# Differential attention of a hybrid block: scores of two heads in one burst, small tiles turned by DMA, and another order of the second half's projections

## The chip, the cores and the metric

The kernel runs on one core of a Trainium2 chip. Its metric is the device time of one execution in microseconds (us). The profile is one execution taken by the hardware profiler. Its engines are called PE (TensorE, matmuls), PEld (TensorE's weight loads), DVE (VectorE), ACT (ScalarE), POOL (GpSimd) and SP (SyncE, which here only issues DMAs).

## The reference

Two layers work on 272 tokens (16 learned "meta" tokens and 256 of the input) with 1024 features. Each layer has a mixer with three branches, retention (4 heads), HGRN2 (8 heads) and differential attention (8 heads), and a feed-forward part with a short convolution. All projections come from one matrix. The part that matters here, cut:

```python
q = rope(q.reshape(b, l, 2 * DA_HEADS, DA_DH), pos).reshape(b, l, DA_HEADS, 2, DA_DH) * DA_DH ** -0.5
k = rope(k.reshape(b, l, 2 * DA_HEADS, DA_DH), pos).reshape(b, l, DA_HEADS, 2, DA_DH)
...
    s = jnp.einsum('bqhmd,bkhmd->bhmqk', qb, k)
    p = jax.nn.softmax(jnp.where(allowed, s, MASK_VALUE), axis=-1)
    w = p[:, :, 0] - lam * p[:, :, 1]
    return jnp.einsum('bhqk,bkhe->bqhe', w, v)
...
o = _rms(o) * subln_g.astype(F32) * (1.0 - lambda_init)
...
y_b = jnp.einsum('blnc,ncd->blnd', branches, w_branch.astype(F32))
y = jnp.sum(gates * y_b, axis=2)
```

So each of eight heads has two score maps (m = 0, 1) with 64 features each. Their softmaxes are subtracted with a factor, and the difference weighs 128 values per head.

## The kernel before, in words

**Main stream.** Activations lie with features on the partitions and the 272 tokens along the columns (258 in most of layer 1, whose first 14 tokens are needed only as keys). Every projection is a stream of 128x128 weight tiles. `products` (L926) takes a pair of output tiles (16 weight tiles) at a time. Each weight tile is cut by `_Weights.next` (L652) into a high part `whi` (cast by ACT) and a rest `wlo` (subtraction on DVE), and costs three matmuls (L953 to L955): high by high, low by high, high by low. Weights come in chunks of eight tiles over SP's queue into three `wraw` buffers; `whi` and `wlo` have four buffers each.

**Order of the main stream.** `ORDER` (L65) lists the pairs of every layer by name: hq, hf, hi, hg for HGRN2, rq, rk, rv, rg for retention, dq, dk, dv for attention, m0 to m2 for the branch gates, b0 to b2 for the branch products, wo, fi, fo. Marks stand between them: "+daa" and "+dab" are the places where the work of attention's first and second half (four heads each) joins, "!da" is the place by which it is meant to be done, "*b0" to "*b2" split a branch's output into high and low parts (tiles b0hi, b0lo and so on). Before the change the second half's part reads dq, dq, b0, b0, dk, dk, dv, dv, "+dab".

**Side work.** All else is added to a planner (`_Plan`, L356) as operations with an engine, an estimated cost and a key (the wanted place, in units of main stream time). `behind` (L1476) gathers the operations of one job, `in_turn` makes buffers of a tag be taken in the job's order, and `settle` (L1491) spreads the keys of the jobs from their joining to the mark. `behind(..., 2, 8)` lets a job begin after the operation eight from the end of the job three places before it in the chain. `order` (L456) then runs a greedy simulation, one queue for each engine, and fixes the order of instructions. A main matmul is never moved before another; side matmuls go between them. An operation starts at most 12 units before its key.

**Buffers.** The main products use two PSUM tiles ("main"). Side matmuls use two banks of tag "bank" and two of tag "acc". Tags of small buffers: "two_a", "two_b" (score maps, 2 each), "wts" (2), "vsrc" (4, shared by the 16-bit planes "apart" and "turned" and by the values before they are turned), "dm" (2).

**Attention.** `da_first` (L1362) computes the first 16 rows of all four heads at once: scores "ds" from a block-diagonal q, softmax, both maps combined into `w`, and a matmul "wt" with a constant that turns and sums the maps into `dw`. `da_head` (L1392) does one head: it takes a "wts" buffer a1 and copies its part of `dw` there, computes the scores of 256 rows into two "bank" tiles (four matmuls over 64 rows each, two of 272 and two of 144 columns, L1405 to L1411), adds the mask and takes the maximum on DVE, exponentials on ACT, combines the maps on DVE, turns the 32-bit result by two DMA transposes (ACT copies the 16-bit halves apart, SP issues the two transposes, ACT copies them back to a1), and multiplies by the values ("do"). The last 16 columns of the two row blocks are gathered in `dt`. `da_tail` (L1458) turns `dt` by a TensorE transpose ("wt"), and multiplies by the tail values `dvs`. Then b2hi and b2lo are made of the output `da`.

**Tails of the values.** `tail_tokens` (L1020) turns the last 16 tokens of rv, hi and dv by a TensorE transpose into a bank ("vm"), and ACT copies them to "vs". It is called five times in a layer (rv once, hi twice, dv twice).

Of the kernel before, what the change touches and what calls it, by code (L numbers as in the profile page):

```python
# [15 lines left out]
U16 = mybir.dt.uint16  # L16
# [5 lines left out]
P = 128  # L22
# [36 lines left out]
def _pairs(name, lo, hi):  # L59
# [16 lines left out]
    + _pairs("dq", 2, 4) + _pairs("b0", 0, 2) + _pairs("dk", 2, 4) + _pairs("dv", 2, 4)  # L76
    + [("+dab", 0)]
# [617 lines left out]
def _trace(ctx, tc, plan, a, depth, probe):  # L695
# [323 lines left out]

    def tail_tokens(tails):  # L1020

        pm = bank("vm")
        pe.transpose(pm[:, :P], tails, ident)
        vs = temp(P, "vs", 4)
        act.activation(vs, pm[:, :P], AF.Copy)
        return vs
# [40 lines left out]
    for li in range(depth):  # L1067
# [294 lines left out]
        def da_first(b):  # L1362
# [11 lines left out]
            pool.memset(w, 0.0)  # L1374
            s = bank("ds")
# [10 lines left out]
            wt = bank("wt")  # L1386
            pe.matmul(wt[:, : 4 * META], w, const[:, C_SUM:C_MAP], start=True, stop=True)
            st[f"dw{b}"] = temp(4 * META, "am", 3)
            act.activation(st[f"dw{b}"], wt[:, : 4 * META], AF.Copy)
            st[f"dt{b}"], st[f"do{b}"] = (temp(P, n, 1).rearrange("p (g h t) -> p g h t", g=2, h=4) for n in ("dt", "dot"))  # L1390

        def da_head(b, hd):  # L1392
            q, k, vt, out = st[f"dq{b}"], st[f"dk{b}"], st[f"dvt{b}"], st[f"da{b}"]
            scale = DA_DH ** -0.5

            a1 = temp(T + P + TAIL, "wts")
            act.activation(a1[:, :META], st[f"dw{b}"][:, hd * META : (hd + 1) * META], AF.Copy)
            tiles = ((META + P, T, 0), (META, META + P, T))
            sb = [temp(2 * T, tag) for tag in ("two_a", "two_b")]
            ss = [bank("ds") for _ in range(2)]  # L1400
            red = temp(12, "dm")
            nm, sm, cf = (red[:, 4 * i : 4 * i + 4].rearrange("p (t m) -> p t m", m=2) for i in range(3))


            def scores():  # L1405
                for q0, nk, at in tiles:
                    for m in range(2):
                        half = slice(64 * m, 64 * m + 64)
                        nc.tensor.matmul(ss[m][:, at : at + nk], q[half, hd, q0 : q0 + P], k[half, hd, :nk], start=True, stop=True)  # L1409

            plan.add("pe", scores, 0.95, [x[:, : T + P + META] for x in ss], [q[:, hd, :], k[:, hd, :]])  # L1411
            plan.hold(*sb, a1)
            for i, (q0, nk, at) in enumerate(tiles):
                mask = const[:, C_MASK + T - nk : C_MASK + T]
                for m in range(2):
# [175 lines left out]
        for name, j in ORDER:  # L1591
# [8 lines left out]
            elif name in ("+daa", "+dab"):  # L1600
# [3 lines left out]
                for hd in range(4):  # L1604
                    behind(lambda: da_head(b, hd), "da", 2, 8)
# [174 lines left out]
```

## Time and profile before

| | before |
|---|---|
| median of 3 runs (lowest to highest) | 1275.9 us (1275.59 to 1276.77) |
| the profiled execution | 1275.23 us |
| its span, first to last instruction | 1273.4 us |
| mean granted TensorE clock | 0.999 |
| ACT, whi: cast of a chunk of 1024 columns | 1056 ns, 399 of them |
| DVE, wlo: rest of a chunk | 1239 ns, 399 of them |
| DMA transposes issued by SP | 86 |
| weight loads issued by SP, 512 KB each | 402 |

In a row of groups stand the source line, engine and operation, then the tile written and the tiles read (buffer numbers left out), the shape, the count, busy time in us and mean ns of one, and the idle time of the engine just before them with what ended it. L633 is the line of the helper through which all side work is recorded, so side work is told apart by its tiles. In a row of a timeline stand start and duration in us. A matmul of 32-bit data over 128 rows appears as two records, a main matmul or a transpose as one. Ends of matmuls are modelled, starts are recorded. In a row of waits stand the total, the number and the longest.

### The profile page before, as it was taken

The numbers are of one execution on the slowest core, as the hardware profiler recorded it, in microseconds if no ns is written. First come the engines' busy times: TensorE is split into PE (matmuls) and PEld (weight loads), VectorE is DVE, ScalarE is ACT, GpSimd is POOL, SyncE is SP. The second block draws the span as 40 slices with busy tenths as digits, with TensorE's granted clock in tenths as the row PEclk, the third lists the DMA queues.
The fourth block names the chain that finished last, engine by engine and source line by source line (L and its number), as shares of the span: only waits on it lengthen the run. The fifth ranks groups of instructions, "written<-read, shape, count | busy, mean of one in ns | idle before, by whom it ended". The sixth has DMA issues, their size and how long they took to land.

```text
span 1273.4 us, 28668 instructions
## 1 busy us (share of the span) xinstructions
PE 1264.0 (99%) x11626; PEld 1242.9 (98%) x11626; DVE 964.7 (76%) x1669; ACT 886.0 (70%) x1638; POOL 113.3 (9%) x89
## 2 busy tenths in 40 slices
PE   9999999999999999999999999999999999999998
PEld 8999999999999999999999999999999999999986
DVE  6787587898776789786576875869987867898854
ACT  6766677758798576665456567877588975787643
POOL 2000031201111000000010000411011120000000
PEclk9999999999999999999999999999999999999999
DMA  8655547655746546556555545576557466476663
GB/s 269 197 167 158 160 149 227 165 169 147 213 132 208 182 150 199 178 170 190 176 182 182 167 144 187 149 217 186 166 147 227 146 209 196 150 224 204 208 197 108
DMA packets 103444, 229.29 MB, mean 180 GB/s; under 512 B 49552, under 2 KB 49680, under 8 KB 103312
## 3 DMA queue, kind: packets, MB, share of 16 engines
q1 hardware_dynamic: 103024, 226.94, 57.1%
q8 instruction: 91, 1.49, 0.5%
q10 hardware_dynamic: 288, 0.52, 0.1%
q14 instruction: 41, 0.34, 0.1%
HBM read 216.16 MB, written 1.05 MB: 171 GB/s over the span
## 4 chain that ended last, share of the span: by engine, by line
PE 98%; DVE 1%; ACT 0%; DMA 0%; issue 0%; SPq 0%; ACTq 0%
PE main L953 28%; PE main L954 28%; PE main L955 28%; PE fo L1566 2%; PE fo L1564 2%; PE fo L1565 2%; PE lev L1160 1%; PE fi L955 1%; PE fi L954 1%; PE fi L953 1%; PE ds L1409 1%; PE s L633 0%; DMA h<-in_h 0%; PE do L633 0%; PE ro L633 0%; PE px L633 0%
## 5 line engine op out<-in xcount | busy, mean ns | idle before, releaser
L953 PE MATMUL main<-xh,whi 128*128 128x272 f32 (+1 forms) x2240 | 644.1, 288 | 1.6 <-ACT whi L633 1.1
L633 DVE TENSOR_TENSOR wlo<-wraw,whi 128x1024 fp32r<-128x1024 f32 (+1 forms) x411 | 500.2, 1222 | 182.0 <-ACT whi L633 180.5
L955 PE MATMUL main<-xh,wlo 128*128 128x272 f32 (+1 forms) x2240 | 636.8, 284 | 0.4 <-DVE wlo L633 0.4
L954 PE MATMUL main<-xl,whi 128*128 128x272 f32 (+1 forms) x2240 | 636.5, 284 | 0.0
L633 ACT ACTIVATE whi<-wraw 128x1024 fp32r<-128x1024 f32 (+1 forms) x411 | 426.2, 1041 | 202.3 <-PE main L954 99.4
L953 PEld LDWEIGHTS main<-xh,whi 128*128 128x128 f32 x2240 | 421.8, 188 | 2.7 <-ACT whi L633 1.3
L955 PEld LDWEIGHTS main<-xh,wlo 128*128 128x128 f32 x2240 | 421.7, 188 | 1.1 <-DVE wlo L633 0.9
L954 PEld LDWEIGHTS main<-xl,whi 128*128 128x128 f32 x2240 | 421.8, 188 | 0.7 <-issue 0.6
L633 POOL PARTITION_ALL_REDUCE hr<-hsq x36 | 75.1, 2106 | 448.8 <-ACT hsq L633 329.1
L633 DVE SCALAR_TENSOR_TENSOR two_b<-main,small,two_b 128x256 f32<-128x256 f32 (+2 forms) x128 | 54.4, 484 | 27.4 <-ACT two_b L633 27.3
L633 ACT ACTIVATE two_b<-main,small 128x272 f32<-128x272 f32 (+1 forms) x64 | 33.1, 566 | 26.8 <-PE main L955 26.5
L953 PE MATMUL main<-ghi,whi 128*128 128x272 f32 x176 | 50.8, 289 | 0.0
L954 PE MATMUL main<-glo,whi 128*128 128x272 f32 x176 | 50.6, 287 | 0.0
L955 PE MATMUL main<-ghi,wlo 128*128 128x272 f32 x176 | 50.3, 286 | 0.0
L953 PE MATMUL main<-b0hi,whi 128*128 128x272 f32 (+1 forms) x128 | 37.4, 292 | 0.0
L953 PE MATMUL main<-b1hi,whi 128*128 128x272 f32 (+1 forms) x128 | 37.1, 290 | 0.0
L953 PE MATMUL main<-yhi,whi 128*128 128x272 f32 (+1 forms) x128 | 36.4, 284 | 0.0
L955 PE MATMUL main<-yhi,wlo 128*128 128x272 f32 (+1 forms) x128 | 36.3, 284 | 0.0
L954 PE MATMUL main<-b0lo,whi 128*128 128x272 f32 (+1 forms) x128 | 36.3, 284 | 0.0
L954 PE MATMUL main<-ylo,whi 128*128 128x272 f32 (+1 forms) x128 | 36.3, 284 | 0.0
L955 PE MATMUL main<-b1hi,wlo 128*128 128x272 f32 (+1 forms) x128 | 36.3, 284 | 0.0
L954 PE MATMUL main<-b1lo,whi 128*128 128x272 f32 (+1 forms) x128 | 36.3, 284 | 0.0
(275 smaller groups left out, 2144.3 us busy)
## 6 DMA issues: line engine op xcount, KB each, us to landing
wraw<-in_w SPq DMA_DIRECT2D x402, 512.0 KB, 3.8
turned<-apart SPq DMA_TRANSPOSE x86, 2.5
h<-in_h SPq DMA_DIRECT2D x4, 272.0 KB, 5.4
dec<-in_dec SPq DMA_DIRECT2D x2, 544.0 KB, 5.7
wraw<-in_w SPq DMA_DIRECT2D x4, 256.0 KB, 5.0
const<-in_const SPq DMA_DIRECT2D x1, 937.0 KB, 7.7
gain<-in_gl SPq DMA_DIRECT2D x1, 512.0 KB, 4.4
out<-y ACTq DMA_DIRECT2D x2, 256.0 KB, 2.6
```

The lines of the kernel that those rows point to most:

```text
L633: self.plan.add(self.name, lambda: f(*args, **kw), cost, outs, ins, kind)
L953: nc.tensor.matmul(o, wh, hi, start=first, stop=False)
L954: nc.tensor.matmul(o, wh, lo, start=False, stop=False)
L955: nc.tensor.matmul(o, wl, hi, start=False, stop=last)
L1160: nc.tensor.matmul(o, keys, x, start=True, stop=True)
L1409: nc.tensor.matmul(ss[m][:, at : at + nk], q[half, hd, q0 : q0 + P], k[half, hd, :nk], start=True, stop=True)
L1564: nc.tensor.matmul(o, gh, wh, start=first, stop=False)
L1565: nc.tensor.matmul(o, gl, wh, start=False, stop=False)
L1566: nc.tensor.matmul(o, gh, wl, start=False, stop=end)
```

## The change

- `flip` is new: it turns a 128x128 tile of 32-bit values with two ACT copies that take the 16-bit halves apart, two DMA transposes issued by SP, and two ACT copies back. It needs one "vsrc" buffer.
- `tail_tokens` uses it in place of the TensorE transpose and the copy from PSUM. `da_first` uses it in place of the matmul "wt", with a DVE addition of the two maps behind it. `da_tail` uses it in place of the TensorE transpose. That makes 18 flips: ten in `tail_tokens`, four in `da_first`, four in `da_tail`.
- `da_head` becomes `da_pair`: the scores of two heads are one operation of eight matmuls (planned at 1.75 in place of 0.95 for one head) into two "bank" and two "acc" tiles. The maxima of both heads follow, then `da_rest` for each head. The "wts" buffer a1 is taken in `da_rest`, after the maps are combined, and no longer before the scores.
- `ORDER`: the second half reads dv, dv, dq, dq, dk, dk, "+dab", b0, b0.

```diff
--- before.py
+++ after.py
@@ -73,8 +73,8 @@
     + _pairs("dq", 0, 2) + _pairs("dv", 0, 2)
     + _pairs("dk", 0, 2)
     + [("+daa", 0), ("*b0", 0), ("!ret", 0)]
-    + _pairs("dq", 2, 4) + _pairs("b0", 0, 2) + _pairs("dk", 2, 4) + _pairs("dv", 2, 4)
-    + [("+dab", 0)]
+    + _pairs("dv", 2, 4) + _pairs("dq", 2, 4) + _pairs("dk", 2, 4)
+    + [("+dab", 0)] + _pairs("b0", 0, 2)
     + _pairs("b0", 2, 4) + _pairs("m1", 0, 4)
     + [("*b1", 0)]
     + _pairs("b1", 0, 4)
@@ -1017,12 +1017,23 @@
             act.activation(halves(top[2][:, cols].unsqueeze(1), i), turned[:, i, 1:2, :], AF.Copy)
         split(top[0][:, cols], top[1][:, cols], whole)
 
+    def flip(out, x):
+
+        t = planes("turned", 2 * P)
+        apart, turned = (t[:, i].rearrange("p (i x) -> p i x", i=2) for i in range(2))
+        halves = lambda t, i: t.bitcast(U16).rearrange("p (x two) -> p x two", two=2)[:, :, i]
+        for i in range(2):
+            act.activation(apart[:, i], halves(x, i), AF.Copy)
+        for i in range(2):
+            sync.dma_start(turned[:, i].rearrange("p (b x) -> p b x", x=P), apart[:, i], transpose=True)
+        for i in range(2):
+            act.activation(halves(out, i), turned[:, i], AF.Copy)
+
     def tail_tokens(tails):
 
-        pm = bank("vm")
-        pe.transpose(pm[:, :P], tails, ident)
         vs = temp(P, "vs", 4)
-        act.activation(vs, pm[:, :P], AF.Copy)
+        plan.key += 1.0
+        flip(vs, tails)
         return vs
 
     def inverse(r, sq, n):
@@ -1372,6 +1383,7 @@
                 half = slice(64 * m, 64 * m + 64)
                 act.activation(qs.rearrange("p (h m q) -> p h m q", h=4, m=2)[half, :, m, :], q[half, :, :META], AF.Copy)
             pool.memset(w, 0.0)
+            turned = x[:, T : T + P]
             s = bank("ds")
             pe.matmul(s[:, : 4 * META].rearrange("p (h k) -> p h k", h=4), qs, k[:, :, :META], start=True, stop=True)
             dve.tensor_tensor_reduce(out=p, in0=s[:, : 4 * META], in1=const[:, C_FIRST:C_SUM], scale=1.0,
@@ -1383,40 +1395,48 @@
 
             dve.tensor_reduce(out=w[:, :META], in_=p.rearrange("p (h k) -> p k h", h=4), axis=mybir.AxisListType.X, op=ADD)
             ts(w[:, :META], w[:, :META], cf, None, MUL)
-            wt = bank("wt")
-            pe.matmul(wt[:, : 4 * META], w, const[:, C_SUM:C_MAP], start=True, stop=True)
+            flip(turned, w)
+            maps = turned.rearrange("p (h m q) -> p h m q", h=4, m=2)
             st[f"dw{b}"] = temp(4 * META, "am", 3)
-            act.activation(st[f"dw{b}"], wt[:, : 4 * META], AF.Copy)
+            tt(st[f"dw{b}"].rearrange("p (h q) -> p h q", h=4), maps[:, :, 0, :], maps[:, :, 1, :], ADD)
             st[f"dt{b}"], st[f"do{b}"] = (temp(P, n, 1).rearrange("p (g h t) -> p g h t", g=2, h=4) for n in ("dt", "dot"))
 
-        def da_head(b, hd):
-            q, k, vt, out = st[f"dq{b}"], st[f"dk{b}"], st[f"dvt{b}"], st[f"da{b}"]
+        def da_scores(b, heads):
+            q, k = st[f"dq{b}"], st[f"dk{b}"]
+            banks = [[bank("ds") for _ in range(2)], [acc_bank("ds") for _ in range(2)]]
+            sb = [[temp(2 * T, tag) for tag in ("two_a", "two_b")] for _ in heads]
+            tiles = ((META + P, T, 0), (META, META + P, T))
+
+            def scores():
+                for hd, ss in zip(heads, banks):
+                    for q0, nk, at in tiles:
+                        for m in range(2):
+                            half = slice(64 * m, 64 * m + 64)
+                            nc.tensor.matmul(ss[m][:, at : at + nk], q[half, hd, q0 : q0 + P], k[half, hd, :nk], start=True, stop=True)
+
+            plan.add("pe", scores, 1.75, [x[:, : T + P + META] for ss in banks for x in ss],
+                     [x[:, hd, :] for x in (q, k) for hd in heads])
+            plan.hold(*sum(sb, []))
+            return [(ss, p, temp(12, "dm")) for ss, p in zip(banks, sb)]
+
+        def da_pair(b, heads):
             scale = DA_DH ** -0.5
-
-            a1 = temp(T + P + TAIL, "wts")
-            act.activation(a1[:, :META], st[f"dw{b}"][:, hd * META : (hd + 1) * META], AF.Copy)
             tiles = ((META + P, T, 0), (META, META + P, T))
-            sb = [temp(2 * T, tag) for tag in ("two_a", "two_b")]
-            ss = [bank("ds") for _ in range(2)]
-            red = temp(12, "dm")
-            nm, sm, cf = (red[:, 4 * i : 4 * i + 4].rearrange("p (t m) -> p t m", m=2) for i in range(3))
-
-
-            def scores():
-                for q0, nk, at in tiles:
-                    for m in range(2):
-                        half = slice(64 * m, 64 * m + 64)
-                        nc.tensor.matmul(ss[m][:, at : at + nk], q[half, hd, q0 : q0 + P], k[half, hd, :nk], start=True, stop=True)
-
-            plan.add("pe", scores, 0.95, [x[:, : T + P + META] for x in ss], [q[:, hd, :], k[:, hd, :]])
-            plan.hold(*sb, a1)
-            for i, (q0, nk, at) in enumerate(tiles):
-                mask = const[:, C_MASK + T - nk : C_MASK + T]
-                for m in range(2):
-                    cols = slice(at, at + nk)
+            pairs = [(i, m, slice(at, at + nk)) for i, (_, nk, at) in enumerate(tiles) for m in range(2)]
+            lanes = da_scores(b, heads)
+            parts = [[red[:, 4 * i : 4 * i + 4].rearrange("p (t m) -> p t m", m=2) for i in range(3)] for _, _, red in lanes]
+            for (ss, sb, _), (nm, _, _) in zip(lanes, parts):
+                for i, m, cols in pairs:
+                    mask = const[:, C_MASK + T - (cols.stop - cols.start) : C_MASK + T]
                     dve.tensor_tensor_reduce(out=sb[m][:, cols], in0=ss[m][:, cols], in1=mask, scale=1.0,
                                              scalar=-3e38, op0=ADD, op1=ALU.max, accum_out=nm[:, i, m : m + 1])
-            ts(nm, nm, -scale, None, MUL)
+                ts(nm, nm, -scale, None, MUL)
+            for hd, (_, sb, _), (nm, sm, cf) in zip(heads, lanes, parts):
+                da_rest(b, hd, sb, nm, sm, cf, tiles)
+
+        def da_rest(b, hd, sb, nm, sm, cf, tiles):
+            vt, out = st[f"dvt{b}"], st[f"da{b}"]
+            scale = DA_DH ** -0.5
             for i, (q0, nk, at) in enumerate(tiles):
                 for m in range(2):
                     p = sb[m][:, at : at + nk]
@@ -1428,6 +1448,8 @@
                 ts(p1, p1, cf[:, i, 1:2], None, MUL)
                 stt(p0, p0, cf[:, i, 0:1], p1, MUL, ADD)
             w = sb[0]
+            a1 = temp(T + P + TAIL, "wts")
+            act.activation(a1[:, :META], st[f"dw{b}"][:, hd * META : (hd + 1) * META], AF.Copy)
             apart, turned = planes("apart", 3 * P), planes("turned", 3 * P)
             halves = lambda t, i: t.bitcast(U16).rearrange("p (x two) -> p x two", two=2)[:, :, i]
             for i in range(2):
@@ -1458,11 +1480,11 @@
         def da_tail(b):
 
             o, out = st[f"do{b}"].rearrange("p g h t -> p (g h t)"), st[f"da{b}"]
-            wt = bank("wt")
-            pe.transpose(wt[:, :P], st[f"dt{b}"].rearrange("p g h t -> p (g h t)"), ident)
+            turned = temp(P, "tails")
+            flip(turned, st[f"dt{b}"].rearrange("p g h t -> p (g h t)"))
             w = temp(P, "tw")
             blocks = lambda t: t.rearrange("p (h t) -> p h t", t=TAIL)
-            tt(blocks(w), pair(wt[:, P - TAIL : P], 8), blocks(const[:, C_OWN : C_OWN + P]), MUL)
+            tt(blocks(w), pair(turned[:, P - TAIL : P], 8), blocks(const[:, C_OWN : C_OWN + P]), MUL)
             x = acc_bank("do")[:, :P]
             pe.matmul(x, st[f"dvs{b}"], w, start=True, stop=True)
             tt(o, o, x, ADD)
@@ -1601,8 +1623,8 @@
                 b = "ab".index(name[3])
                 st[f"da{b}"] = slot4("da")
                 behind(lambda: da_first(b), "da", 2)
-                for hd in range(4):
-                    behind(lambda: da_head(b, hd), "da", 2, 8)
+                for g in range(2):
+                    behind(lambda: da_pair(b, (2 * g, 2 * g + 1)), "da", 2, 8)
                 behind(lambda: da_tail(b), "da", 2)
             elif name[0] == "!":
                 settle(name[1:])
```

## The prediction

> **What bounds the kernel now.** I read first the page's busy shares and the chain that ended last, then the costliest groups with the idle time before them, then the timeline of TensorE around single interruptions of its main stream.
>
> ```profile
> span 1273.4 us, 28668 instructions
> ...
> PE 1264.0 (99%) x11626; PEld 1242.9 (98%) x11626; DVE 964.7 (76%) x1669; ACT 886.0 (70%) x1638; POOL 113.3 (9%) x89
> ...
> PE 98%; DVE 1%; ACT 0%; DMA 0%; issue 0%; SPq 0%; ACTq 0%
> ...
> L953 PE MATMUL main<-xh,whi 128*128 128x272 f32 (+1 forms) x2240 | 644.1, 288 | 1.6 <-ACT whi L633 1.1
> ...
> L955 PE MATMUL main<-xh,wlo 128*128 128x272 f32 (+1 forms) x2240 | 636.8, 284 | 0.4 <-DVE wlo L633 0.4
> ```
>
> 98% of the chain is TensorE, and the largest groups of its stream stood idle for 1.6 and 0.4 us in all. So waits hide nothing that could be won: a change gains what it takes off TensorE's own work, and loses what it makes TensorE wait. What an interruption costs is read from start to start, since the ends are modelled:
>
> ```profile
> 279.20 0.29 PE L955 MATMUL main<-b0hi,wlo 128*128 128x272 f32 x1
> 279.42 0.97 PE L1409 MATMUL ds<-dk,dq 64*128 64x272 f32 x8
> 280.32 0.39 PE L953 MATMUL main<-b0hi,whi 128*128 128x272 f32 x1
> 280.55 0.29 PE L954 MATMUL main<-b0lo,whi 128*128 128x272 f32 x1
> 280.68 0.29 PE L955 MATMUL main<-b0hi,wlo 128*128 128x272 f32 x1
> ```
>
> Undisturbed, a main matmul starts 0.124 us after the one before (280.55 to 280.68 and on). From 279.20 to 280.55 are 1.35 us where two such steps, 0.25, would do: the scores of one head cost the stream **1.10 us**.
>
> **The scores, two heads in one burst.** The matmuls stay: four for a head, each in two records (x8). What may go is a fixed part of the burst. The same burst, asked for from a later moment, gives the starts inside it; beside it stands a burst of four plain matmuls of 144 columns over all 128 rows:
>
> ```profile
> 279.75 0.64 PE L1409 MATMUL ds<-dk,dq 64*128 64x272 f32 x6
> 279.98 0.41 PE L1409 MATMUL ds<-dk,dq 64*128 64x144 f32 x4
> ...
> 139.32 0.29 PE L955 MATMUL main<-xh,wlo 128*128 128x272 f32 x1
> 139.44 1.14 PE L633 MATMUL px<-hq,hf 128*128 128x144 f32 x8
> 140.55 0.29 PE L954 MATMUL main<-xl,whi 128*128 128x272 f32 x1
> ```
>
> The plain burst costs 1.23 - 0.25 = 0.98 us for eight passes of 144 columns, 0.12 each, and next to nothing for entering and leaving. The score passes run two at a time, one on each half of the rows (eight records are left at 279.42, six at 279.75, four at 279.98). Their columns need 2 x 0.23 (279.75 to 279.98) + 2 x 0.12 = 0.70 us. The remaining **0.40** is the change of shape: 0.10 before the first pass (0.22 instead of 0.12 after 279.20), 0.10 more in the first pass (0.33 to the next pair instead of 0.23), 0.10 before the first main matmul (280.32 instead of 279.98 + 0.24) and 0.10 before the second. A burst of two heads pays it once. If instead the passes only overlap badly, a pair saves nothing; so the bounds are 0 and 0.40 a pair, and I take 0.40, because the starts within the burst show the steady 0.23. Two heads then take 1.80 instead of 2.20, eight times: **3.2 us**. The change adds a wait here: the burst needs all four side banks and the score buffers of two heads at once, and behind it on TensorE stands the main stream. The group of the scores below shows 0.0 idle before it now, since the planner places a burst where it expects its banks free; I take 0 again, and count a misjudged one with rival two.
>
> **The small tiles turned by DMA.** These leave TensorE, with their counts in records and one lone example of two of the forms:
>
> ```profile
> L1409 PE MATMUL ds<-dk,dq 64*128 64x272 f32 x64 | 11.7, 441 | 0.0
> L633 PE MATMUL vm<-const,tails 128*128 128x128 f32 x10 | 2.7, 272 | 0.0
> L633 PE MATMUL wt<-const,wts 128*128 128x64 f32 x8 | 1.3, 246 | 0.0
> L633 PE MATMUL wt<-const,dt 128*128 128x128 f32 x4 | 1.1, 271 | 0.0
> ```
> ```profile
> 391.90 0.29 PE L955 MATMUL main<-xh,wlo 128*128 128x272 f32 x1
> 392.04 0.27 PE L633 MATMUL wt<-const,dt 128*128 128x128 f32 x1
> 392.27 0.29 PE L954 MATMUL main<-xl,whi 128*128 128x272 f32 x1
> ...
> 348.26 0.29 PE L955 MATMUL main<-xh,wlo 128*128 128x272 f32 x1
> 348.39 0.33 PE L633 MATMUL wt<-const,wts 128*128 128x64 f32 x2
> 348.74 0.29 PE L954 MATMUL main<-xl,whi 128*128 128x272 f32 x1
> ```
>
> The 64 records of 272 columns are 16 heads. A transpose costs 0.37 - 0.25 = 0.12 us, fourteen of them (vm 10, dt 4) 1.7 us; the matmul with two records 0.48 - 0.25 = 0.23 us, four of them 0.9 us. Together **2.6 us**. In their place each of 18 flips puts two copies apart, two DMA transposes and two copies back:
>
> ```profile
> L633 ACT ACTIVATE apart<-two_a 128x128 uint16<-128x128 uint16 x32 | 9.3, 295 | 0.0
> L633 ACT ACTIVATE apart<-turned 128x256 uint16<-128x256 uint16 x48 | 23.3, 486 | 3.8 <-DMA turned<-apart 3.8
> L633 ACT ACTIVATE wts<-turned 128x384 uint16<-128x384 uint16 x32 | 20.2, 634 | 1.8 <-DMA turned<-apart 1.8
> L633 ACT ACTIVATE vs<-vm 128x128 f32<-128x128 f32 x10 | 2.7, 265 | 1.0 <-PE vm L633 1.0
> ...
> turned<-apart SPq DMA_TRANSPOSE x86, 2.5
> ...
> sum 200.00, PE 200.00 PEld 196.62 DVE 160.50 ACT 153.95 POOL 28.59; mean PE 10.00 PEld 9.83 DVE 8.02 ACT 7.70 POOL 1.43
> ...
> ACT whi L633 <- PE main L954: 99.4, 79, 2.6
> ```
>
> A copy back of 128 columns is not in the trace; from 486 and 634 ns, 148 ns for each 128 columns, I estimate 338 ns. A flip costs ACT 2 x 0.295 + 2 x 0.338 = 1.27 us, less 0.27 where an eviction goes: some 20 us over the whole kernel, on an engine with 70%. Six flips a layer fall into the attention stretch (225 to 425 us, the row "sum": ACT 154 of 200 us), some 6.5 us more there. The cover is that the weights' casts on ACT are ahead of TensorE: 79 times they waited for TensorE to free a buffer, 99.4 us in all. SP gets 36 transposes beside 86, in one queue with the weights' loads; a load queued behind a transpose that waits for ACT's copy is late by that wait, and behind it wait whi, wlo and, with the buffers used up, TensorE. I take 0 for both while the casts stay ahead; if they don't, it is rival two. The copies that move with the weights' buffer change neither number nor size.
>
> **The order.** dv, dq, dk in a row and the two b0 pairs after the join change no matmul. The join of the second half comes two pairs, 2 x 16 x 3 x 0.124 = 11.9 us, earlier in the stream.
>
> **Sum.** 3.2 + 2.6 = 5.8 us off TensorE. The profiled execution took 1275.23 us (span 1273.4 and 1.8 around it), so 1269.4; the median of the three runs lies 0.7 higher, 1275.9, so **1270.1 us**.
>
> **Rival one, on the other side: attention ends too late for b2.** In the layers' third branch (m2, then b2) TensorE needs the second half's last tile, and before it was ready only just:
>
> ```profile
> 407.68 1.29 DVE L633 TENSOR_TENSOR b2lo<-da,b2hi 128x1088 fp32r<-128x1088 f32 x1 [0.29 <-ACT b2hi L633]
> 410.89 0.29 PE L954 MATMUL main<-b2lo,whi 128*128 128x272 f32 x1
> ...
> 1038.96 1.23 DVE L633 TENSOR_TENSOR b2lo<-da,b2hi 128x1032 fp32r<-128x1032 f32 x1 [0.22 <-ACT b2hi L633]
> 1041.24 0.28 PE L954 MATMUL main<-b2lo,whi 128*128 128x258 f32 x1
> ```
>
> The first b2 matmul that reads that tile is the ninth triple, so the slack was 410.89 - 408.97 = 1.9 us in layer 0 and 1041.24 - 1040.19 = 1.05 in layer 1. A flip lies in the chain of a half twice (first rows' map, last rows' map). It takes 0.59 + 2.5 + 0.68 = 3.8 us against transpose and eviction of 0.27 + 0.27; 3.2 longer, 6.4 for both. If nothing else moved, TensorE would wait 6.4 - 1.9 = 4.5 and 6.4 - 1.05 = 5.4 us, 9.9 in all, and what it had saved before would at worst be waited away too: 1275.9 + 9.9 - 5.8 = 1280 to 1285 us. It decides once the chain ends more than 1.9 and 1.05 us later against the main stream. The Trainium skill (VectorE: DVE Perf Modes, Rules for kernel authors) says to turn a 128x128 tile on TensorE if its result may go to PSUM, and by the DMA crossbar otherwise, with 390 against 1309 ns for 16-bit data (The three transpose paths). By that an estimate of a flip of two planes is 2.2 us longer, and the waits 2.5 and 3.4 us; the trace agrees in direction (2.5 us to landing against 0.27). Against this rival speaks what the chain waited for:
>
> ```profile
> 319.20 0.42 POOL L633 MEMSET wts<- 128x128 f32 x2
> 336.79 0.31 ACT L633 ACTIVATE da<-tw 128x128 f32<-128x128 f32 x1
> 349.52 0.91 PE ds L1409 x8
> ```
>
> The second half's first rows began only when a weights' buffer came free (319.20), their scores' map was ready only just before 349.52, 12.4 us after the first half had ended (337.1). With the buffer taken at the join, dv's copies gone from that stretch, and the join 11.9 us earlier, those 12.4 us can close. The chain: +6.4 for the first half, -12.4, +3.2 for the last flip (the second half's first flip lies beside the first half): 2.8 us earlier, against 2.9 us that TensorE is faster in a layer. The slack stays about what it was, so a wait is possible but not the rule: 0.17.
>
> **Rival two: weights or banks late.** In the stretch with ACT at 77% some chunks come late when flips take ACT and SP at a bad moment, or a burst of two heads finds a bank taken. Stalls of 0.5 to 1 us, two or three in a layer, give back 2 to 4 us: 1272 to 1274. For it: flips need ACT twice with a DMA between. Against it: the 99.4 us above, and that dv's copies leave the fullest part. 0.17.
>
> **Rival three: the pairing saves nothing**, the burst of two heads taking 2.2 us: 1270.1 + 3.2 = 1273.3. The starts inside the burst speak against it. 0.05.
>
> **How the numbers follow.** Forecast 0.61 (1269 to 1271.5), rivals 0.17, 0.17, 0.05. The range 1268.8 to 1275.0 holds the forecast, rivals two and three, and leaves rival one out. A measurement of this kernel tells 0.2%, 2.55 us, from no change, so faster is below 1273.35: the forecast 0.61, two thirds of rival two 0.11, half of rival three 0.02, together 0.74. The rest of two and three, 0.09, and 0.02 of a mild rival one are the same: 0.11. Slower: 0.15.
>
> **What would show it.** Right: eight bursts "ds" with x16 in place of sixteen with x8, each 1.80 us start to start in the main stream; no vm and wt group on PE, so 22 records fewer there (x11604); 122 transposes; TensorE's groups still idle for 1 to 3 us in all. Rival one: idle time before L954 or L953 of b2 released by DVE b2lo, in both layers. Rival two: L953 or L955 waiting for ACT whi or DVE wlo between 225 and 425 us. Rival three: a pair's burst at 2.2. The forecast is wrong if TensorE waits over 3 us more than before in sum, whatever for.

## The result, and the profile after

| | before | after |
|---|---|---|
| median of 20 runs (lowest to highest) | 1275.95 us (1275.23 to 1279.5) | 1278.23 us (1275.32 to 1281.12) |
| ratio to before, 95% interval | | 1.0014 [1.0008, 1.002] |
| profiled execution, its span | 1275.23, 1273.4 us | 1275.95, 1274.2 us |

The changed kernel is slower by 2.3 us in the median (by 0.1 to 0.2%, as the interval has it), where 5.8 us faster was forecast. From the page of the changed kernel (span; busy time and instructions of the engines; chain that ended last; the first and third group with the idle time before them; the transposes, with the us to landing):

```profile
span 1274.2 us, 28739 instructions
...
PE 1259.8 (99%) x11604; PEld 1239.8 (97%) x11604; DVE 962.6 (76%) x1673; ACT 899.9 (71%) x1696; POOL 117.9 (9%) x89
...
PE 82%; issue 5%; DVE 5%; DMA 4%; ACT 2%; POOL 1%; SPq 1%; ACTq 0%; DVEq 0%; POOLq 0%
...
L953 PE MATMUL main<-xh,whi 128*128 128x272 f32 (+1 forms) x2240 | 642.5, 287 | 1.6 <-ACT whi L633 1.6
...
L955 PE MATMUL main<-xh,wlo 128*128 128x272 f32 (+1 forms) x2240 | 636.8, 284 | 1.8 <-DVE wlo L633 1.7
...
turned<-apart SPq DMA_TRANSPOSE x86, 3.0
...
turned<-turned SPq DMA_TRANSPOSE x36, 2.4
```

The work did leave: 22 TensorE instructions fewer, 36 transposes more. The timeline of the changed kernel shows one burst of two heads (start, duration):

```profile
301.27 0.28 PE L955 MATMUL main<-b0hi,wlo 128*128 128x272 f32 x1
301.49 1.68 PE L1415 MATMUL ds<-dk,dq 64*128 64x272 f32 x16
303.10 0.39 PE L953 MATMUL main<-b0hi,whi 128*128 128x272 f32 x1
303.33 0.28 PE L954 MATMUL main<-b0lo,whi 128*128 128x272 f32 x1
```

From 301.27 to 303.33 are 2.06 us where two steps, 0.25, would do: 1.81, where 1.80 was forecast. All eight bursts lie at 1.79 to 1.81. So the 5.8 us came off TensorE. But its share of the chain fell from 98% to 82%: others ended last now. The waits of TensorE in the changed kernel (engine and line, what it waited for; us in all, times, longest):

```profile
PE main L955 <- DVE wlo L633: 2.5, 4, 0.8
PE main L953 <- ACT whi L633: 1.6, 3, 0.8
PE ro L1062 <- DVE ho L633: 1.3, 2, 0.9
...
PE ro L1062 <- ACT tw L633: 1.0, 1, 1.0
```

**The balance.** I measured each interruption of TensorE's stream from start to start, and took off what its matmuls need undisturbed. What is left, counted where it is over 0.12 us, was 2.9 us before and is 9.7 us after. So 1273.4 - 5.8 + (9.7 - 2.9) = 1274.4, and the span is 1274.2. Of the 20 executions of the changed kernel, 16 are longer than the profiled one, and the median is 2.3 us above it; where they lose that, no trace shows. The eleven with a mean granted clock under 0.999 have a median of 1279.02, the other nine 1276.99, so stretches at a lower clock (last section) may be a part of it.

**Who made TensorE wait.** The longest stop for weights, in the changed kernel's timeline (other engines' rows and most of the main stream are left out):

```profile
313.74 1.20 DVE L633 TENSOR_TENSOR wlo<-wraw,whi 128x1024 fp32r<-128x1024 f32 x1
...
317.21 3.75 SPq L633 DMA_TRANSPOSE turned<-apart  x2
...
319.94 0.29 ACT L633 ACTIVATE turned<-dt 128x128 uint16<-128x128 uint16 x1
...
321.07 2.45 SPq L633 DMA_TRANSPOSE turned<-turned  x2
...
323.61 6.69 SPq L633 DMA_DIRECT2D wraw<-in_w  x4
...
327.62 1.06 ACT L633 ACTIVATE whi<-wraw 128x1024 fp32r<-128x1024 f32 x1 [2.31 <-DMA wraw<-in_w]
327.63 0.28 PE L955 MATMUL main<-b0hi,wlo 128*128 128x272 f32 x1
...
328.71 1.23 DVE L633 TENSOR_TENSOR wlo<-wraw,whi 128x1024 fp32r<-128x1024 f32 x1 [3.40 <-ACT whi L633]
```

SP's rows follow one another. From 317.21 to 323.52 they are four transposes, the last two a flip's, whose second plane ACT copied apart at 319.94; four loads follow in one run. Two more transposes stand before these, from 314.18 on: the first four belong to the two heads of a pair, and of the 9.3 us the flip's share is 2.45. A run of six transposes between loads occurs nowhere in the kernel before (four at most), nor in e1, which has no flips (two at most), nor in e8, which has no pairs (four at most). The buffer of the first had been free for 8.67 us (from the end of the wlo that emptied it, 314.94), those of the next two for 6.28 and 4.54. ACT stands 2.31 us for the first of them, then casts, and DVE starts its rest at 328.71; TensorE, which had used up its last cut chunk at 327.63, stood 0.98 us and then 0.91. The same chunk's load came 0.02 us after its buffer was free in the kernel before, 1.8 in e1 and 0.5 in e8.

The longest stop of all is at retention's output (ro), and starts in the same queue:

```profile
225.94 1.24 SPq L633 DMA_TRANSPOSE turned<-turned  x1
...
227.22 6.76 SPq L633 DMA_DIRECT2D wraw<-in_w  x4
...
231.31 1.06 ACT L633 ACTIVATE whi<-wraw 128x1024 fp32r<-128x1024 f32 x1 [2.62 <-DMA wraw<-in_w]
232.28 0.26 ACT L633 ACTIVATE tw<-ro 128x128 f32<-128x128 f32 x1
...
232.59 0.40 PE L1062 MATMUL ro<-kt,rvt 128*128 128x272 f32 x1 [1.02 <-ACT tw L633]
```

The transposes of a flip (the second is shown) stand before the loads. The first load's buffer had been free for 7.48 us (3.8 in the kernel before). ACT stood 2.62 us for that load, cast it, and only then made the small copy tw that TensorE waited for, 1.28 us from start to start. Not every stop is the queue's: at 988 us (0.98 us, on wlo) the load had landed 6.7 us before its cast; ACT had stood 2.11 us for a flip's landing and then worked off both heads of a pair first.

**What had covered this.** Here are the waits of ACT's casts in the second layer's attention stretch (840 to 1065 us), first before, then after. "<- PE" is a cast that waited for TensorE to free a buffer (it was ahead), "<- DMA" one that waited for its load (it was behind):

```profile
ACT whi L633 <- DMA wraw<-in_w: 15.3, 12, 3.1
ACT whi L633 <- PE main L954: 10.0, 11, 1.8
```
```profile
ACT whi L633 <- DMA wraw<-in_w: 19.0, 21, 2.9
ACT whi L633 <- PE main L954: 2.7, 3, 1.7
```

The same rows for 425 to 840 us, between the layers' attention, where only two of the 18 flips and none of the pairs fall; before, then after:

```profile
ACT whi L633 <- PE main L954: 57.4, 40, 2.6
```
```profile
ACT whi L633 <- PE main L954: 60.8, 41, 2.6
```

In the first layer's stretch (225 to 425 us) the casts that were ahead fell from 16.2 to 8.7 us and those behind rose from 9.9 to 14.9. So 57.4 of the 99.4 us that I took for cover lay where next to nothing needed it. For each chunk I also took from the trace the time from the end of its cut (wlo) to the first matmul that reads it: in 200 to 425 and 840 to 1065 us, 10 of 138 chunks were ready less than 2 us ahead before, and 33 of 137 after. The time by which loads were issued later than their buffers came free adds up to 88 us before and 162 us after.

### The profile page after: what moved, and what is told of

Its sections match the earlier page's. It is cut to its first block, busy times and chain, and to the rows that moved or that the text cites. A ratio compares the mean times of both kernels' runs of the same rounds, so it can differ in the third digit from the quotient of the medians.

```text
span 1274.2 us, 28739 instructions
## 1 busy us (share of the span) xinstructions
PE 1259.8 (99%) x11604; PEld 1239.8 (97%) x11604; DVE 962.6 (76%) x1673; ACT 899.9 (71%) x1696; POOL 117.9 (9%) x89
## 4 chain that ended last, share of the span: by engine, by line
PE 82%; issue 5%; DVE 5%; DMA 4%; ACT 2%; POOL 1%; SPq 1%; ACTq 0%; DVEq 0%; POOLq 0%
PE main L953 23%; PE main L955 23%; PE main L954 23%; DMA wraw<-in_w 4%; DVE wlo L633 2%; PE fo L1588 2%; PE fo L1587 2%; PE fo L1586 2%; POOL hr L633 1%; PE lev L1171 1%; PE fi L955 1%; PE fi L953 1%; PE fi L954 1%; ACT whi L633 1%; DVE two_c L633 1%
## 5 line engine op out<-in xcount | busy, mean ns | idle before, releaser
L633 POOL PARTITION_ALL_REDUCE hr<-hsq x36 | 77.9, 2183 | 431.8 <-ACT hsq L633 412.4
L955 PE MATMUL main<-b0hi,wlo 128*128 128x272 f32 (+1 forms) x128 | 36.3, 284 | 0.0
```

The costliest lines, as they stand in the source:

```text
L633: self.plan.add(self.name, lambda: f(*args, **kw), cost, outs, ins, kind)
L955: nc.tensor.matmul(o, wl, hi, start=False, stop=last)
```

## The experiments

All ratios are to the kernel before, run on the same chip beside them. "Waits" are TensorE's in the profiled execution, by the method above; "sum" is 1273.4 minus the work that the parts take off, plus waits over 2.9.

| kernel | parts | median us | ratio [95%] | waits | sum | span |
|---|---|---|---|---|---|---|
| e5 | pairs | 1274.35 | 0.9991 [0.9981, 1.0] | 4.3 | 1271.6 | 1271.5 |
| e6 | order | 1276.32 | 1.0005 [0.9996, 1.0013] | 3.4 | 1273.9 | 1274.2 |
| e2 | flips | 1292.16 | 1.0134 [1.0121, 1.0147] | 20.2 | 1288.1 | 1291.8 |
| e1 | pairs, order | 1276.1 | 1.0007 [0.9998, 1.0015] | 7.5 | 1274.8 | 1276.7 |
| e8 | flips, order | 1275.94 | 1.0004 [0.9995, 1.0013] | 5.2 | 1273.1 | 1272.5 |
| e3 | pairs, flips | 1281.54 | 1.0046 [1.0034, 1.0058] | 12.5 | 1277.2 | 1278.7 |
| after | all three | 1278.23 | 1.0014 [1.0008, 1.002] | 9.7 | 1274.4 | 1274.2 |
| e4 | all, 18 fewer transposes | 1277.67 | 1.002 [1.001, 1.0031] | 10.6 | 1275.3 | 1276.9 |
| e11 | all, tails on TensorE | 1278.33 | 1.0022 [1.0013, 1.0031] | 9.8 | 1275.7 | 1276.5 |
| e17 | all, replanned | 1279.53 | 1.0033 [1.0021, 1.0046] | 11.9 | 1276.6 | 1276.6 |
| e9 | all, lead 8 | 1274.72 | 0.9992 [0.9983, 1.0] | 7.8 | 1272.5 | 1272.2 |
| e13 | all, lead 8 later | 1272.68 | 0.9976 [0.9966, 0.9986] | 5.6 | 1270.3 | 1270.3 |
| e14 | all, the load's lead only | 1273.77 | 0.9985 [0.9976, 0.9994] | 8.0 | 1272.7 | 1274.6 |
| e12 | pairs, lead 8 | 1274.48 | 0.9989 [0.9981, 0.9998] | 4.7 | 1272.0 | 1273.1 |
| e16 | pairs, lead 8 later | 1272.19 | 0.9972 [0.9962, 0.9982] | 3.9 | 1271.2 | 1271.5 |
| e7 | none, replanned | 1277.39 | 1.0015 [1.0006, 1.0024] | 4.3 | 1274.8 | 1275.2 |
| e15 | none, lead 8 later | 1278.05 | 1.0018 [1.0009, 1.0027] | 5.0 | 1275.5 | 1275.4 |
| e18 | flips, lead 8 later | 1291.31 | 1.0117 [1.0098, 1.0137] | 19.8 | 1287.7 | 1290.8 |

The sum meets the span within 0.6 us in ten rows, and is 0.8 to 3.7 short in eight; five of these (e1, e2, e3, e4, e18) hold a stretch at half clock (the last section shows how).

### The parts one by one (e1, e2, e3, e5, e6, e8)

**e1**: the changed kernel with the 18 flips taken back.

```diff
-        plan.key += 1.0
-        flip(vs, tails)
+        pm = bank("vm")
+        pe.transpose(pm[:, :P], tails, ident)
+        act.activation(vs, pm[:, :P], AF.Copy)
```
(and so for the matmuls "wt" of `da_first` and `da_tail`)

> The changed kernel with the 18 flips taken back (transposes and the matmul wt on TensorE again); pairs, the late weights' buffer and the new order stay. Theory S (a DMA transpose holds SP's queue for 1.2 us whatever its size, the weights' loads behind it come late): the stalls go, the 3.2 us of the pairs stay, 1272.7 us; loads issued after their buffer is free sum to about 88 us again instead of 162. Rival A (ACT's added copies make the casts late): 1272.7 too. Rival O (the new order or the pairs crowd DVE and ACT): stays at 1276 or above, with stalls of 4 us or more left.

It gave 1276.1, a miss of 3.4. The loads' delay behind free buffers fell to 76 us, as theory S had it, and the waits for weights from 4.1 to 1.9 us, but it held one new wait.

```profile
PE do L1063 <- DVE da L633: 3.3, 1, 3.3
```

The product of a head waited for an acc bank that the output's norm still read, and the clock fell after it (below).

**e2**: the kernel before with the flips alone.

```diff
+    def flip(out, x):
...
-        pm = bank("vm")
-        pe.transpose(pm[:, :P], tails, ident)
+        flip(vs, tails)
```

> The kernel before with the 18 flips only; heads one by one and the old order. S and A: 2.6 us off TensorE, 4 to 7 us of new stalls, so 1277 to 1280 us, TensorE waiting for ACT whi and DVE wlo. O: no stalls, 1273.3 us.

1292.16, 12 us above the expected and the slowest of these eight. Its waits, and its timeline at the longest:

```profile
PE main L953 <- ACT b2hi L633: 5.8, 1, 5.8
PE main L953 <- ACT whi L633: 1.9, 1, 1.9
PE main L954 <- DVE b2lo L633: 1.8, 2, 1.1
```
```profile
1052.47 0.28 PE L955 MATMUL main<-b2hi,wlo 128*128 128x258 f32 x1
...
1057.13 0.31 ACT L633 ACTIVATE da<-tw 128x128 f32<-128x128 f32 x1 [0.41 <-DVE tw L633]
1057.47 1.06 ACT L633 ACTIVATE b2hi<-da 128x1032 fp32r<-128x1032 f32 x1
...
1058.59 0.58 PE L953 MATMUL main<-b2hi,whi 128*128 128x258 f32 x1 [5.84 <-ACT b2hi L633]
```

This is the prediction's rival one, near its priced size (5.4 us for this layer): the attention's last tile is written at 1057.13, when TensorE has stood since 1052.75. In the other layer its stops at b2 are 1.5 us, where 4.5 was priced.

**e3**: the changed kernel with the old ORDER.

```diff
-    + _pairs("dv", 2, 4) + _pairs("dq", 2, 4) + _pairs("dk", 2, 4)
-    + [("+dab", 0)] + _pairs("b0", 0, 2)
+    + _pairs("dq", 2, 4) + _pairs("b0", 0, 2) + _pairs("dk", 2, 4) + _pairs("dv", 2, 4)
+    + [("+dab", 0)]
```

> The changed kernel with the old order (dq, dq, b0, b0, dk, dk, dv, dv, join). S and A: the stalls stay, since the flips stay: 1276 to 1281 us. O: if the order crowds the engines, the stalls go and 1270 to 1272 us come out.

1281.54: the pairs recover 10.6 of the flips' 16.8 us in the old order, where alone they are worth 1.1.

**e5**: the kernel before with `da_pair` and the late a1 of the change, and nothing else. **e6**: with the new ORDER alone. **e8**: with flips and new ORDER, heads one by one.

```diff
-                for hd in range(4):
-                    behind(lambda: da_head(b, hd), "da", 2, 8)
+                for g in range(2):
+                    behind(lambda: da_pair(b, (2 * g, 2 * g + 1)), "da", 2, 8)
```

> The kernel before with the scores of two heads in four banks and the weights' buffer taken at the join, in the order of before and with every small tile turned on TensorE. Theory P (the pairing's own waits: four banks held for two heads make the next matmul or the next norm wait): the 3.2 us of work go and as much comes back as waits of TensorE at do and ds, so 1275 to 1278. Theory F (only the turning by DMA, in whatever order, brings the waits): 1275.3 minus 3.2, 1272.1.

> The kernel before in the new order (second half's v, q and k in a row, the first half's heads one by one), nothing turned by DMA, no pairs. No work is taken or added. Theory O (the new order crowds the weights' splitting and its loads against the attention): 1277 to 1279, with TensorE waits at main on whi, wlo or at do on da. Theory F (the order is harmless without the turning by DMA): 1275.3.

> The kernel before with the small tiles turned by DMA and in the new order, without pairs (heads one by one). Work taken off TensorE: 2.6 us. If the new order alone cures the late attention of the second batch (the wait of 5.8 us on b2hi seen with the turning by DMA in the old order): 1275 to 1280, and the pairs are worth their 3.2 us beside it. If it is the pairs, which end the attention sooner, that cure it: 1285 or more.

e5 kept 1.1 of its 3.2 us in the median, between the theories P and F (its own profile shows 1.4 us more waits than before and a span 1.9 shorter); its interval leaves out 3.2. e6 is no different from before: the order by itself is harmless, and theory O falls. e8 shows that the order alone cures the late second batch: 1275.94 against 1292.16. What the flips take off TensorE, 2.6 us, is nearly all waited away again (5.2 - 2.9 = 2.3), most of it at retention's output:

```profile
PE ro L1062 <- DVE ho L633: 0.9, 1, 0.9
PE ro L1062 <- ACT tw L633: 0.8, 1, 0.8
```

These stops are not in e1. Put together the parts do worse than their effects say: the pairs, worth 1.1 alone, give nothing where flips and order are in place (after lies 2.3 above its runs of before, e8 0.5; the two intervals overlap, but a gain of 3.2 is far outside). What the two do to the weights differs. The loads' delay is the flips': 124 to 177 us in every kernel that has all or some of them and loads from SP, 76 to 93 in every kernel without. But delay alone did not make chunks late: less than 2 us ahead in the attention stretches were 10 chunks before, 12 in e8 (delay 154), 17 in e5, 16 in e1, and 33 with flips and pairs together. Each of these counts is of one profile.

### Fewer transposes, other queues (e4, e10, e11)

**e4**: each flip's two planes by one DMA transpose.

```diff
-        for i in range(2):
-            sync.dma_start(turned[:, i].rearrange("p (b x) -> p b x", x=P), apart[:, i], transpose=True)
+        sync.dma_start(turned, apart.rearrange("p i x -> p (i x)"), transpose=True)
```

> The changed kernel with each flip's two planes in one DMA transpose of 256 columns instead of two of 128. ACT's copies are the same. S: SP is held 18 x 1.2 = 22 us less, about half of the 7 us of new stalls go, 1273 to 1275.5 us. A and O: unchanged, 1277 to 1278.5 us.

The three waits at ro fell from about 3 us to about 0.6, and the loads' delay from 162 to 124 us, but other waits came in attention, and the time stayed: 1277.67.

**e10**: the weights' loads issued by POOL.

```diff
-    weights = _Weights(plan, wp, a["w"], act, dve, sync)
+    weights = _Weights(plan, wp, a["w"], act, dve, _Engine(plan, nc.gpsimd, "pool", 0.06, 4 / 360e3))
```

> The changed kernel with the weights' loads issued by POOL instead of SP, so no load stands behind a transpose. Theory S: the waits at main on whi and wlo (4.1 us) and at ro on tw and ho (3.1 us, behind late splits) mostly go, about 1273. Theory A: they stay, 1277 to 1279. If POOL's own issue is the slower one, the loads come late from the start and it is slower than 1280.

1353.26, ratio 1.0608 [1.0594, 1.0623], with 67.5 us of TensorE waits. It tells nothing for or against SP's queue, because more changed than the queue: an issue kept POOL busy for 0.53 us where it held SP for 0.33 (the loads landed as soon, 3.8 against 3.9 us in the median), the loads' delay grew to 226 us, and the transposes landed later (4.1 and 3.9 us in place of 3.0 and 2.4). Which of these cost the time is open. The page's DMA queues: the loads have left SP's queue (q1), and POOL's busy time rose from 117.9 to 328.5 us.

```profile
PE 1286.2 (95%) x11604; PEld 1257.5 (93%) x11604; DVE 969.7 (72%) x1673; ACT 896.8 (66%) x1696; POOL 328.5 (24%) x495
...
q0 software_dynamic: 58208, 211.84, 48.5%
q1 hardware_dynamic: 50320, 16.29, 6.8%
```

**e11**: the tails' tokens on TensorE again, the rest of the flips as changed (the edit of e1 in `tail_tokens` alone).

> The changed kernel with the tails' tokens turned on TensorE again (the 14 vm transposes), while the differential tiles stay turned by DMA. 14 times 0.12, 1.7 us of work, come back. Theory S (the 28 extra transposes of the retention part hold back loads there): the three waits at ro (3.1 us, of which 0.5 would be there anyway) go, so 1278.2 plus 1.7 minus 2.6, 1277. If these waits have nothing to do with the tails' flips: 1280.

1278.33. Only ten transposes, 1.2 us of work, came back here, not the 14 and 1.7 us of the expectation (x11614 on TensorE). The waits at ro fell to under 0.4 us, as theory S has it, but as in e4 others took their place (1.4 us at 730 us, about 1 at 960): the time is not better.

### The loads' lead (e9, e12 to e18)

The planner gives a load and its split a key 6 units before their first matmul (LEAD). **e9** raises that to 8. **e13** does so from chunk 13 on (counted from 0). **e14** does it for the load alone. **e15** is e13's step in the kernel before, **e12** e9's and **e16** e13's in e5, **e18** e13's in e2. **e7** and **e17** change another constant (MARGIN 12 to 13) in the kernels before and after.

```diff
-LEAD = 6.0
+LEAD = 8.0
...
-            self.plan.key = due - LEAD
+            self.plan.key = due - (LEAD if c > 12 else 6.0)
```
(e14 has below the `dma_start` one line more, `self.plan.key = due - 6.0`)

> The changed kernel with one constant of the planner raised (LEAD 6 to 8 us): each weights' load and its split are given an earlier place on SP, ACT and VectorE, so loads stand ahead of more of the transposes. Theory S (the loads wait on SP behind transposes that wait for their copies): the waits at main on whi and wlo (4.1 us in the changed kernel) mostly go, 1274 to 1276. Theory A (ACT and VectorE have too much to do at these places, whoever loads): no gain, 1277 to 1279. Theory R (every re-plan gets its own 1 to 4 us of waits): anywhere from 1274 to 1280, with the waits at other places.

> The changed kernel with the weights' lead of 8 us instead of 6 from the 13th chunk on (the first 40 us keep 6, where 8 alone brought 2.0 us of waits on xl). Theory S (loads held on SP behind transposes are what the change loses by): 8 us everywhere gave 1274.7, less the 2.0: 1272.7. Theory R (the gain was chance): 1275 to 1279.

> As e13, but only the load on SP gets the earlier place; the split on ACT and VectorE keeps its lead of 6. Theory S with SP alone: as e13, 1272.7. If it is the split's place on ACT and VectorE that matters: the changed kernel's 1278.

e9 was 3.5 us faster than the changed kernel, although the start now lost 2.0 us; e13, without that loss, came to 1272.68, the number that theory S had worked out, and beats both kernels. Its waits of TensorE in the attention stretches, first 225 to 425, then 840 to 1065 us:

```profile
PE main L955 <- DVE wlo L633: 0.4, 1, 0.4
```
```profile
PE do L1062 <- DVE dm L633: 0.3, 1, 0.3
PE ro L1062 <- DVE ho L633: 0.3, 1, 0.3
PE main L955 <- DVE wlo L633: 0.2, 1, 0.2
```

But it did not come by theory S's mechanism: the chunks ready less than 2 us ahead are 27 of 138, not many fewer than 33, and the loads' delay behind a free buffer did not fall, 177 us against 162. The queue is not shorter, and why TensorE stands less is not shown. In e14 the loads alone gave 4.5 of the 5.5 us in the median. Its profile, of an execution 2.7 us above its median, shows stops like those of the changed kernel (8.0 us); so that SP's part is the larger is the times' word, and no trace shows how.

> The kernel before with one constant of the planner changed (MARGIN 12 to 13): the same work, the same order of parts, other places for the small operations. Theory R (the plan of before happens to be almost free of TensorE waits, and any other plan costs 1 to 4 us of them): 1276.5 to 1279. Theory F (the plan is robust, only the turning by DMA brings waits): 1275.3 within 0.5.

> The kernel before with the same lead of 8 from the 13th chunk on. Its loads wait 88 us in all for a free SP against 162 of the changed kernel, and it has 2.9 us of TensorE waits of which about 1 on weights: theory S 1275.0, no gain above 0.8. If a lead of 8 is good for any plan: 1272 to 1273, and what e13 gains says nothing of the change.

> The changed kernel with MARGIN 13 instead of 12 (the step that cost the kernel before 1.9 us), lead unchanged. Theory R (what e13 gained is what another plan gives by chance): somewhere between 1273 and 1280. Theory S: loads stay behind the transposes, so 1277 to 1280, and not below 1276.

> The turning by DMA alone in the old order (1292.2), with the lead of 8 from the 13th chunk on. If its 16.8 us come from loads held on SP: 1276 to 1282. If they come from the attention of the second batch ending too late for the weights of b2 (5.8 us on b2hi), which no earlier load cures: 1288 or more.

The controls. e17: another plan of the changed kernel is no better, 1279.53. e15: in the kernel before the same lead loses 2.4 us, where I had expected no change. e7: MARGIN 13 costs the kernel before 1.9. So theory R has its share: a plan of this kernel can lose about 2 us with no work added, and that of before is a good one. Three plans of the changed kernel with a longer lead (e9, e13, e14) gain 3.5 to 5.5 us, and two others without it (e4, e17) gain 0.6 and lose 1.3, which speaks against chance alone, though the three share one constant. e18: the lead does not cure the late second batch (4.3 us on b2hi remain), as expected: that loss is not the loads'.

> The kernel before with the pairs and the weights' buffer at the join alone (old order, nothing more turned by DMA), with LEAD 8 instead of 6. The pairs alone gave 1274.35, with 4.3 us of TensorE waits of over 0.12 us, one of 1.06 on wlo. If earlier loads remove the weights' waits: 1272 to 1273, faster than before and after. Theory R: 1273 to 1277 with other waits.

> Pairs and late buffer alone, old order, lead 8 from the 13th chunk on. Pairs alone gave 1274.35, with lead 8 everywhere 1274.5 of which some 1.4 were new waits at the start: 1273.0; the work alone would be 1272.3.

e16 is the fastest kernel of the study by its median, 1272.19, with its 3.2 us of work kept; its interval and e13's overlap. So flips and new order add no gain over pairs alone, even when the loads have their lead. And the lead's gain cannot be put down to the flips' transposes alone: from e5 to e16, which have none of them, it is 2.2 us (with lead 8 from the start, e12, it is none).

## Why the prediction was wrong

- **What bounds the kernel**: right. The 18 sums above rest on it, and ten of them meet the span within 0.6 us.
- **Scores of two heads**, the work: right, 1.79 to 1.81 against 1.80; eight bursts, 3.2 us.
- **Small tiles off TensorE**, the work: right. No vm and wt group is left, and the balance closes with 2.6 us.
- **"I take 0 for both while the casts stay ahead"** (the flips' work on ACT and on SP): this step failed. Taking the flips out of the changed kernel (e1) brings the loads' delay from 162 to 76 us; without the pairs (e8) the flips still wait away 2.3 of their 2.6 us, most of it at ro. The 99.4 us of casts that were ahead looked like ample cover, but 57.4 of them lay between the attention stretches. In these two stretches 26.2 us were ahead, and 25.2 us of casts were already behind their loads.
- **"I take 0 again" for the burst of two heads**: this step failed too. With the pairs the waits grew from 5.2 (e8) to 9.7 us, more than the 3.2 us that they take off, and in the median they gave nothing. It was less the banks, which the prediction feared, than the weights: TensorE's waits on whi and wlo rose from 0.6 us in e8 to 4.1. Alone (e5) the pairs brought 1.4 us of waits, most of it one of 1.1 us for weights at 1011 us. A wait for an acc bank of 3.3 us stands in e1; the changed kernel's rows have none.
- **Both together**: the waits grew by 6.8 us, more than the 5.8 of work, and over the 3 us that the prediction named as its sign of being wrong. The mechanism stood as rival two, priced at 2 to 4 us and a chance of 0.17; its price was too low.
- **Order at 0**: right by itself (e6). It was worth far more beside the flips: 16.3 us (e2 lies 16.8 above its runs of before, e8 0.5).
- **Rival one**: its mechanism was real, and in one layer its price; e2 shows it in the old order, and in the new order, as the text argued, it does not come.
- **What remains open**: where the executions longer than the profiled one lose their 2 us, why the longer lead helps e5 and the changed kernel and not the kernel before, and why flips and pairs together leave so many more chunks short. That loads behind transposes make TensorE stand is shown by the rows at 225 to 233 and 314 to 329 us for these places, and at 988 us ACT's order did it. Flips and the delay of loads go together over all runs, but no experiment took the transposes out of the loads' way and left ACT's copies (e10, meant for it, changed more than that), so the shares of SP and ACT are not known.

## What to carry to other kernels

Cover is a property of a stretch: before an added cost is set to 0, read the waits of the engine that is said to be ahead in just the window where the cost falls, and ask both which waits say "ahead" and which say "behind". When the bound engine is 99% busy, work taken from it comes with a schedule that the other engines must meet sooner, so try the lead of its inputs as a step of its own (8 in place of 6 gained 5.5 us in the changed kernel and lost 2.4 in the one before), and run a control that re-plans with no work changed, since 2 us here was a plan's luck. When two parts are each given a cost of 0, ask what they do in the same place. Take a change of several parts apart and put it together again: here one part cost 16.8 us alone, and next to none beside a second.

## What the runs showed of the hardware

**A stop of TensorE can cost twice.** Granted clock by stretch, in e1 around its wait of 3.3 us (window; length and PE busy with count, then PEld, DVE, ACT, POOL; granted clock; DMA share, GB/s):

```profile
390.00:392.00 2.00, 0.69 (x3) 0.72 (x4) 2.00 (x3) 2.00 (x3) 0.00 (x0) 0.59 0.17 27
392.00:394.00 2.00, 2.00 (x11) 2.00 (x11) 1.67 (x3) 0.69 (x3) 0.65 (x1) 0.50 0.86 266
...
396.00:398.00 2.00, 2.00 (x13) 2.00 (x13) 0.26 (x1) 1.36 (x3) 0.01 (x1) 0.70 0.44 174
398.00:400.00 2.00, 2.00 (x19) 2.00 (x18) 1.36 (x2) 0.80 (x3) 1.90 (x1) 1.00 0.07 8
```

Eleven records in 2 us where 19 fit later: the half clock lasts some 6 us after the stop, so by an estimate from these rows the stop's price is 3.3 us and some 6 x (1 - 11 / 19) = 2.5 more. The windows around the changed kernel's stops of up to 1.3 us all show 1.00. But the length of one stop does not settle it. In e3 the clock fell after a stop of 1.5 us with one of 0.7 behind it:

```profile
328.00:330.00 2.00, 2.00 (x12) 2.00 (x12) 1.62 (x2) 1.96 (x8) 1.16 (x1) 0.56 0.11 22
330.00:332.00 2.00, 2.00 (x12) 2.00 (x12) 0.00 (x0) 1.88 (x7) 0.57 (x2) 0.58 0.80 291
```

That is half clock for some 3.4 us, 1.4 us lost by the same estimate, and about what e3's sum lacks. In e4 it fell after a stop of 1.4 us (0.57 and 0.58 in 1006 to 1010 us); in e15 it stayed at 1.00 after one of 1.5. The Trainium skill (TensorE: Matmul & The Clock Gate, What's actually happening) puts the fall to half clock after at least one idle window of about 3.4 us that runs freely. e1's stop of 3.3 us is near that; e3's and e4's are less than half of it, and there the measurement decides.

**A small DMA transpose holds SP's queue as long as a larger one.** Durations on SP (lowest, median, highest ns; first and last start) in the changed kernel:

```profile
L633 SPq DMA_TRANSPOSE turned<-apart x86: 1177/1228/2517, 119.1 to 1153.5; - x86
L633 SPq DMA_TRANSPOSE turned<-turned x36: 1095/1187/2256, 129.3 to 1018.1; - x36
```

The 36 of 128 columns take 1.19 us, the 86 of 384 and 512 columns 1.23. So the flips put 43 us more on SP's queue; with 18 transposes of 256 columns (e4), at a median of 1.19 us each, half of it.
